# A third probability buffer, a second head-output buffer, raw weights in the keys' tile, and the first keys copied by ScalarE, in a two-layer hybrid attention kernel

## The chip, the cores and the metric

The kernel runs on one core of a Trainium2 chip. Its five engines each work through their own queue in order: TensorE (PE: matrix products, with its weight loads shown as PEld), VectorE (DVE), ScalarE (ACT), GpSimd (POOL) and SyncE (SP), which here only issues DMAs. They wait for one another through semaphores. The metric is the device time of one execution in microseconds (us); lower is better.

## The reference

A backbone of two layers over 512 latent tokens (8 rows of 64) and 256 context tokens, 1024 channels wide. Each layer normalises and modulates its input, projects it once, and runs two attentions side by side: a neighbourhood attention (8 heads of 64, window 8 x 16, relative bias, plus all context keys) and a grouped-query attention (8 query heads, 2 key heads). Each is gated and projected, and both are merged and go through an output projection:

```python
qa = _rmsnorm(hs(a_q, NA_HEADS), q_norm_a)
ka = _rmsnorm(hs(a_k, NA_HEADS), k_norm_a)
a_att = _na_latent(qa, ka, va, cka, cva, rpb, rows)
qb = _rope_2d(_rmsnorm(hs(b_q, GQA_Q_HEADS), q_norm_b), pos_row, pos_col)
b_att = _gqa_latent(qb, k_all, v_all)
# _attend: p = softmax(q k^T / 8); out = p v
# _merge:
o_a = (a_att * silu(a_z)) @ w_o_a
o_b = (b_att * silu(b_z)) @ w_o_b
merged = sigmoid(g_a) * o_a + sigmoid(g_b) * o_b
x_new = x + gate_x * (merged @ w_out)
```

Layer 0 also updates the context tokens (their own attention and projections); layer 1 does not.

## The kernel before

**Products.** Large projections are done to float32 accuracy as three products of rounded parts, high by high, high by low and low by high (L467, L468, L469). A weight tile is loaded raw by SP (256 KB, 128x512), ScalarE casts the high part `whi` (L452, L437), and GpSimd or VectorE subtracts it to get `wlo` (L454, L440). Activations are split in the same way; for the gated attention outputs the parts are `gah`/`gal` and `gbh`/`gbl` (L714 ScalarE, L715 subtraction). Attention products take pairs of float16 tiles.

**Stages of a layer.** Keys, values and queries of the neighbourhood attention; its eight heads; keys, values and queries of the grouped-query attention; its eight heads; then the merge and the output projection. Products of other projections ("fill") are put between the heads' products, so that TensorE has work while the softmax of a head runs elsewhere: gates `zt`/`za`, the first output projection with `w_o_a` (its pieces are emptied from PSUM by VectorE at L750 into `tg`), and, at the end, the second with `w_o_b`.

**The neighbourhood stage.** `na_first(h)` stages head h's keys: `stage_k` copies two halves of 64x1536 float16 values from the large tile `ka` into `kk` (L920, three buffers), and the scores read `kk`. In layer 0 the fill around it is a gate's projection into `za`, whose halves ScalarE (L668) and VectorE (L670) empty.

**The grouped-query stage.** A head has four blocks of 128 queries. For a block TensorE writes scores of 128x768 into PSUM (L928, L929); VectorE finds the maxima and copies the scores into a tile `p` (L1209); ScalarE takes the exponential into `p` (L1210) and casts a float16 part `h` (L898); VectorE (blocks 0 and 2) or GpSimd (blocks 1 and 3) subtracts for the second part (L899); SP transposes both by DMA into `ht` (L903). `p` is free again when L899 is done. In layer 0 a block of context queries follows (L947, `ct`). Then the head's values: twelve products `pst<-ht,vb` (L1226, L1227), a copy and a sum into a tile `ho` (L885, L886), and `zb = zb * ho` (L890). The tile `ho` has one buffer. `divide` (L908, L910, L911) applies the softmax sums. Head h's values come after head h+1's scores, so head 7's come last.

**Buffers.** `NP_GQ = (2, 4)` gives layer 0 two and layer 1 four `p` tiles. Raw weight tiles have three buffers; inside an attention stage every second one comes from an extra set in the stage's pool instead, three buffers in the neighbourhood stages and layer 0's grouped-query stage, two in layer 1's (`raw_tile`, `more_raw`). The grouped-query keys fill only the first half of the large tile `gk`.

**Order.** A scheduler places instructions on every engine from the program text and the buffers, so a change of buffers moves instructions far away from it. No order is written out by hand.

Of the kernel before, what the change touches and what calls it, by code (L numbers as in the profile page):

```python
# [27 lines left out]
STAGE_T = (1, 2)  # L28
NP_GQ = (2, 4)
NH_GQ = (3, 4)  # L30
NT_NA = 2
P_LOG = 9.7
# [42 lines left out]
def hybrid_kernel(es: ExitStack, tc, x, ctx, cvec, w_ada, w_ada0, small, gvec, w_in, w_o_a, w_o_b, w_out,  # L75
# [13 lines left out]
    def nm(s):  # L89
        uid[0] += 1  # L90
        return f"{s}_{uid[0]}"
# [464 lines left out]
    def turn(y, npair, dst, t, perm, g):  # L556
# [10 lines left out]

        todo = []

        def pair(hi, lo, x, g):  # L570
# [67 lines left out]
    def layer(l, hx, nxt, start):  # L638
# [114 lines left out]
        pairs = lambda name: big(name).bitcast(F16).rearrange("p (x j n) -> p x j n", x=2, j=4)  # L753
        kav = pairs("ka")
        k_to = ("k", kav[:, 0], kav[:, 1])
        if first:
# [48 lines left out]
        w = load_w(W, C_AV, 512, KT, mix_lo)  # L805
        za = big("za")
        ti, te = za[:, 0:2048].rearrange("p (h n) -> p h n", h=8), za[:, 2048:3072].rearrange("p (h n) -> p h n", h=8)
        nc.sync.dma_start(ti, bias_int[l].rearrange("h p n -> p h n"))
        nc.sync.dma_start(te, bias_edge[l].rearrange("h p n -> p h n"))

# [6 lines left out]
        for t in range(6):  # L817
            tok_proj(w, 512, a_hx, t, evac_va)
            if t == 3:
# [8 lines left out]
        qav = pairs("qa")  # L828
        w = load_w(W, C_AQ, 512, KT, mix_lo, own=hp["p"])
        fill = fill_chunks(C_AZ, lambda: za, None, True, mix_lo) + fill_chunks(C_BZ, None, zs, True, mix_lo)  # L830
        gates = []
# [4 lines left out]
        for t in range(qt):  # L836
            tok_proj(w, 512, a_hx, t, evac_na(("q", qav[:, 0], qav[:, 1]), True, gq, YB if first else 4))
            if t == 0:
                split_va()
            run(bg, per_bg)  # L840
# [7 lines left out]
        if True:  # L848
# [29 lines left out]
            def head_out(po, e, dst, eng=None, back=None):  # L878

                n = dst.shape[-1]  # L880
                m, o = 64 * e, 64 * (1 - e)
                t1 = att["p"].tile([128, 512], F32, tag="ho", name=nm("ho"), bufs=1)
                a = t1[m:m + 64, :n]
                if back is None:
                    S.copy(a, po[o:o + 64, :n])  # L885
# [4 lines left out]
                (eng or G).tensor_tensor(dst, dst, a, ALU.mult)  # L890
# [25 lines left out]

            def stage_k(src, j, e, to):

                for half in range(2):
                    V.tensor_copy(rows(to, half), rows(src, e)[:, :, j, :])  # L920

            def q_pair(src, e, j):
                return src[:, e, j, :]

            def scores(ps, q, kh, kl, cuts):
# [8 lines left out]
            def ctx_scores(q, kh, kl, ct, late=True):  # L934
# [6 lines left out]
                V.tensor_reduce(mx, pss.rearrange("p (i n) -> p i n", i=2), AX, ALU.max, negate=True)  # L941
                dq = gq_dq if late else na_dq[:, l:l + 1]
                V.tensor_scalar(mx, mx, dq, P_LOG if late else 0.0, ALU.mult, ALU.add)
                p = p_tile()
# [47 lines left out]
            def load_bias(h):  # L992
                nc.sync.dma_start(bint[:, 0:256], b_int[l][h])
                for i in range(2):
                    nc.sync.dma_start(bedg[64 * i:64 * i + 64, 128 * i:128 * i + 128],
                                        b_edge[l][h, 64 * i:64 * i + 64])

            turns = big("ht").bitcast(F16)

            def na_scores(h, q, kh, kl):  # L1000
# [3 lines left out]
                for i in range(4):  # L1004
# [4 lines left out]
                    else:  # L1009
# [11 lines left out]
                    V.tensor_tensor_reduce(p[:, :512], pss, bedg if i == 0 else bint, na_ndq[:, l:l + 1], 3e38,  # L1021
                                           ALU.add, ALU.min, mx[:, 0:1])
# [34 lines left out]
            def pipeline(fill, spread, scores_of, values_of, last=None, bg=[]):  # L1057
# [16 lines left out]
                run(fill, len(fill))  # L1074

            def na_first(h):
                j, e = h // 2, h % 2
                kk = att["p"].tile([128, 2, 768], F16, tag="kk", name=nm("kk"), bufs=3)
                kh, kl = kk[:, 0], kk[:, 1]
# [33 lines left out]
            vbig = big("vb")  # L1113
            g_inv, g_up = vbig[:, 2952:2954], vbig[:, 2954:2956]
            gq_dq, gq_ndq = vbig[:, 2956:2957], vbig[:, 2957:2958]
            g_abs = vbig[:, 1920:2048].rearrange("p (a d) -> p a d", a=2)
            S.copy(g_abs, gbc)
            head_scales(g_abs, g_inv, g_up)
            V.tensor_scalar(gbc[:, 0, :], gbc[:, 0, :], g_up[:, 0:1], None, ALU.mult)
            V.tensor_scalar(gbc[:, 1, :], gbc[:, 1, :], g_up[:, 1:2], 8.0, ALU.mult, ALU.mult)  # L1120
            V.tensor_tensor(gq_dq, g_inv[:, 0:1], g_inv[:, 1:2], ALU.mult)
            V.tensor_scalar(gq_ndq, gq_dq, -1.0, None, ALU.mult)
            V.tensor_scalar(vbig[:, 2950:2951], g_up[:, 0:1], g_up[:, 1:2], -P_LOG, ALU.mult, ALU.mult)

# [7 lines left out]
            vs = vbig[:, 2944:2946]  # L1132
            kbv = hp["p"].tile([128, 2, 1, 768], F16, name=nm("kb"), bufs=1)
            kb_to = ("k", kbv[:, 0], kbv[:, 1])
            gkt = big("gk").bitcast(F16)[:, 0:3072].rearrange("p (e x n) -> p e x n", e=2, x=2)

# [30 lines left out]
            hp["lag"] = 2  # L1167
            qbv = pairs("qb")
            q_to = ("q", qbv[:, 0], qbv[:, 1])
            fill = in_order(gates[n_na:] + o_chunks("a", prepare, evac_a), first)  # L1170
# [8 lines left out]
            for t in range(qt):  # L1179
# [4 lines left out]
                if t in STAGE_T:  # L1184
                    e = STAGE_T.index(t)
                    stage_k(kbv, 0, e, gkt[:, e])

# [7 lines left out]
            if first:  # L1195
                pm["v_for"] = (2,)
            nc.sync.dma_start(zb.rearrange("p (f n) -> p f n", f=4)[:, :, :ntok], zs[:, :, :ntok])
            lift = vbig[:, 2950:2951].to_broadcast([128, 768])

            def gq_scores(q, kh, kl):  # L1200
                ht = att["p"].tile([128, 4, 12, 128], F16, tag="ht", name=nm("ht"), bufs=2)
                r = att["p"].tile([128, 4], F32, tag="r4", name=nm("r4"), bufs=3)
                for i in range(4):
# [4 lines left out]
                    mx = sp.tile([128, 2], F32, tag="mx", name=nm("mx"), bufs=8)  # L1208
                    V.tensor_tensor_reduce(p, pss, lift, gq_ndq, 3e38, ALU.add, ALU.min, mx[:, 0:1])  # L1209
                    S.activation(p, pss, AF.Exp, bias=mx[:, 0:1], scale=gq_dq, accum_out=r[:, i:i + 1])  # L1210
                    turned(p, 768, ht[:, i], G if i in SPLIT_POOL else V)
# [19 lines left out]
            def gq_first(h):  # L1231
                kh, kl = gkt[:, h // 4, 0], gkt[:, h // 4, 1]
                q = q_pair(qbv, h % 2, h // 2)
                ht = gq_scores(q, kh, kl)
# [344 lines left out]
```

## Time and profile before

| | us |
|---|---|
| median of 3 runs | 1122.98 |
| lowest, highest | 1122.5, 1125.72 |
| profiled execution | 1123.93 |
| its span | 1121.6 |
| mean granted TensorE clock | 0.992 |
| DVE, ACT, POOL busy | 784.1, 607.8, 456.8 |

The span is what the trace covers of the profiled execution. In the trace layer 0's neighbourhood heads begin near 153 us, its grouped-query heads end near 538; layer 1's grouped-query heads lie between 930 and 1052. A row of the timeline gives the start, the duration, the engine, the line in the program, the operation, what is written and read, and in brackets how long the engine stood idle before it and what released it. A row of the waits view gives, for one engine and line and one releaser, the idle time in total, the number of waits and the longest.

### The profile page before, as it was taken

Reading aid. Unit: us, or ns where it says so; the run is one execution under the profiler, and the core shown is the slowest. Engines: PE = TensorE matmul, PEld = TensorE weight load, DVE = VectorE, ACT = ScalarE, POOL = GpSimd, SP = SyncE. Lnnn points to the kernel's source line nnn. Section 1 sums busy time; section 2 is a strip of 40 time slices with the busy share of each in tenths; the row PEclk is TensorE's granted clock in tenths of the full one; section 3 lists DMA queues with packets and bytes.
Section 4 is the critical chain, followed back from the end, with each engine's and each line's share of the span. In section 5 each row is a group of like instructions: output and inputs, shape, how many; then the busy total and the mean of one; then the engine's idle time right before and its main releaser. Section 6 shows DMA issues by size and latency. Waiting matters only on the chain. (4 is left out here: it accounts for less than half of the span.)

```text
span 1121.6 us, 16972 instructions
## 1 busy us (share of the span) xinstructions
PE 1073.7 (96%) x5672; PEld 842.3 (75%) x5672; DVE 784.1 (70%) x1667; ACT 607.8 (54%) x1219; POOL 456.8 (41%) x393
## 2 busy tenths in 40 slices
PE   8999989999999999889999999999999998999898
PEld 5688877777888867666888778887666886756687
DVE  4667998976379488656577866477886776677473
ACT  5465448776433566766230274544797436688231
POOL 1054314654245155465322535332554453575421
PEclk8999999999999999989999999999999999999999
DMA  9665334754544499789533533753564437789643
GB/s 358 205 177 170 103 100 102 149 132 100 169 131 131 118 223 204 160 215 245 169 116 102 195 122 95 231 155 109 138 144 115 139 107 189 177 234 233 156 144 93
DMA packets 244464, 178.20 MB, mean 159 GB/s; under 512 B 160285, under 2 KB 210329, under 8 KB 242713
## 3 DMA queue, kind: packets, MB, share of 16 engines
q1 hardware_dynamic: 236896, 162.61, 53.5%
q0 software_dynamic: 2368, 7.87, 2.1%
q10 hardware_dynamic: 5112, 6.66, 1.9%
q8 instruction: 44, 0.72, 0.3%
q14 instruction: 44, 0.35, 0.1%
HBM read 118.86 MB, written 20.47 MB: 124 GB/s over the span
## 5 line engine op out<-in xcount | busy, mean ns | idle before, releaser
L899 POOL TENSOR_TENSOR h<-p,h 128x256 f16<-128x256 f32 (+2 forms) x104 | 109.8, 1062 | 175.0 <-ACT h L898 140.1
L467 PE MATMUL psf<-hx,whi 128*128 128x512 f32 (+1 forms) x360 | 138.9, 386 | 2.6 <-DVE za L670 1.5
L454 POOL TENSOR_TENSOR wlo<-raw,whi 128x512 fp32r<-128x512 f32 x70 | 97.9, 1407 | 97.6 <-ACT whi L452 67.6
L469 PE MATMUL psf<-hx,wlo 128*128 128x512 f32 (+1 forms) x360 | 137.3, 382 | 0.0
L468 PE MATMUL psf<-hx,whi 128*128 128x512 f32 (+1 forms) x360 | 136.7, 380 | 0.0
L468 PE MATMUL psx<-wlo,hx 128*128 128x512 f32 (+1 forms) x328 | 120.8, 369 | 1.3 <-DVE wlo L440 1.3
L467 PE MATMUL psx<-whi,hx 128*128 128x512 f32 (+1 forms) x328 | 120.9, 370 | 0.0
L469 PE MATMUL psx<-whi,hx 128*128 128x512 f32 (+1 forms) x328 | 120.3, 367 | 0.0
L452 ACT CAST whi<-raw 128x512 fp32r<-128x512 f32 x136 | 80.7, 618 | 57.8 <-DMA raw<-in_w_in_dram 33.5
L440 POOL TENSOR_TENSOR wlo<-raw,whi 128x512 fp32r<-128x512 f32 x40 | 54.6, 1367 | 137.5 <-ACT whi L437 99.0
L437 ACT CAST whi<-raw 128x512 fp32r<-128x512 f32 x88 | 54.0, 624 | 91.9 <-PE psx L469 30.4
L540 POOL TENSOR_TENSOR ss<-ss,ehalf 128x8 f32<-128x8 f32 (+2 forms) x40 | 65.8, 1648 | 87.6 <-DVE ss L537 86.2
L898 ACT CAST h<-p 128x256 f16<-128x256 f32 (+2 forms) x136 | 81.7, 616 | 10.5 <-DVE p L857 4.3
L1210 ACT ACTIVATE p<-pss,mx,vb 128x768 f32<-128x768 f32 x64 | 63.4, 993 | 43.7 <-DVE mx L1209 42.4
L1209 DVE CUSTOM_DVE_ANT_0 p<-pss,vb 128x768 f32<-128x768 f32 x64 | 64.2, 1013 | 31.6 <-PE pss L929 26.7
L454 DVE TENSOR_TENSOR wlo<-raw,whi 128x512 fp32r<-128x512 f32 x66 | 69.5, 1061 | 18.9 <-ACT whi L452 18.7
L467 PEld LDWEIGHTS psf<-hx,whi 128*128 128x128 f32 x360 | 67.9, 189 | 16.0 <-ACT zt L668 1.9
L469 PEld LDWEIGHTS psf<-hx,wlo 128*128 128x128 f32 x360 | 67.8, 188 | 12.2
L468 PEld LDWEIGHTS psf<-hx,whi 128*128 128x128 f32 x360 | 68.0, 189 | 11.1
L468 PEld LDWEIGHTS psx<-wlo,hx 128*128 128x128 f32 x328 | 62.0, 189 | 11.8 <-DVE wlo L440 2.2
L467 PE MATMUL psx<-hx,whi 128*128 128x256 f32 (+1 forms) x208 | 69.3, 333 | 0.4 <-DVE za L670 0.4
L469 PEld LDWEIGHTS psx<-whi,hx 128*128 128x128 f32 x328 | 61.9, 189 | 10.1 <-DVE hx L383 0.4
(350 smaller groups left out, 2904.2 us busy)
## 6 DMA issues: line engine op xcount, KB each, us to landing
raw<-in_w_in_dram SPq DMA_DIRECT2D x168, 256.0 KB, 3.1
rawb<-in_w_ada_dram SPq DMA_DIRECT2D x48, 256.0 KB, 3.1
raw<-in_w_out_dram SPq DMA_DIRECT2D x32, 256.0 KB, 2.9
tg<-gs SPq DMA_DIRECT2D x4, 1536.0 KB, 7.3
rawx<-in_w_ada_dram SPq DMA_DIRECT2D x4, 1024.0 KB, 11.4
rawy<-in_w_ada_dram SPq DMA_DIRECT2D x4, 1024.0 KB, 10.7
gs<-zt ACTq DMA_DIRECT2D x16, 256.0 KB, 2.5
raw<-in_w_o_a_dram SPq DMA_DIRECT2D x16, 256.0 KB, 3.2
```

The lines of the kernel that those rows point to most:

```text
L437: S.copy(hi[:, :n], raw[:, :n])
L440: e.tensor_tensor(lo[:, :n], raw[:, :n], F(hi[:, :n]), ALU.subtract)
L452: S.copy(hi, raw)
L454: lo_eng(i).tensor_tensor(lo, raw, F(hi), ALU.subtract)
L467: T.matmul(ps, lhs[0], rhs[0], start=first, stop=False)
L468: T.matmul(ps, lhs[0], rhs[1], start=False, stop=False)
L469: T.matmul(ps, lhs[1], rhs[0], start=False, stop=last)
L540: G.tensor_tensor(ss, ss, ehalf[:, :n], ALU.pow)
L898: S.copy(h[:, 0], p[:, :n])
L899: eng.tensor_tensor(h[:, 1], p[:, :n], h[:, 0], ALU.subtract)
L1209: V.tensor_tensor_reduce(p, pss, lift, gq_ndq, 3e38, ALU.add, ALU.min, mx[:, 0:1])
L1210: S.activation(p, pss, AF.Exp, bias=mx[:, 0:1], scale=gq_dq, accum_out=r[:, i:i + 1])
```

## The change

Five things take effect. Layer 0's grouped-query stage gets three `p` tiles instead of two. In both layers the extra raw weight tiles of that stage are three slices of the unused half of the tile `gk`, no longer tiles of the stage's pool; in layer 1 that is one more than before, and the slices exist before the stage opens. `ho` has two buffers in both attentions. Head 0's two key copies in layer 0 are done by ScalarE (`S.copy`). One small product on `gcol` is split into two. The diff adds another path for `NA_PAIRS` or `GQ_PAIRS` being false; both are true for both layers, so none of it is built. Lines of the changed kernel have other numbers: L946 is the old L920, L980 and L981 the old L928 and L929, L1301 and L1302 the old L1209 and L1210, L771 the old L750.

```diff
-NP_GQ = (2, 4)
+NP_GQ = (3, 4)
+NA_PAIRS = (True, True)
+GQ_PAIRS = (True, True)
...
-                return more_raw["p"].tile([128, 512], F32, tag="rawp", name=nm("raw"), bufs=more_raw["bufs"])
+                return more_raw["p"]()
...
-        V.tensor_tensor(gcol[:, 48:52], gcol[:, 48:52], flat(up), ALU.mult)
+        for l in range(2):
+            if NA_PAIRS[l]:
+                c = 48 + 2 * l
+                V.tensor_tensor(gcol[:, c:c + 2], gcol[:, c:c + 2], up[:, l], ALU.mult)
...
-                t1 = att["p"].tile([128, 512], F32, tag="ho", name=nm("ho"), bufs=1)
+                t1 = att["p"].tile([128, 512], F32, tag="ho", name=nm("ho"), bufs=2 if (na_pairs if att["w"] == 512 else gq_pairs) else 1)
...
-            def stage_k(src, j, e, to):
+            def stage_k(src, j, e, to, eng):
 
                 for half in range(2):
-                    V.tensor_copy(rows(to, half), rows(src, e)[:, :, j, :])
+                    eng(rows(to, half), rows(src, e)[:, :, j, :])
...
-                more_raw["p"], more_raw["bufs"] = att["p"], 3 if width == 512 or first else 2
+                pool, turn = att["p"], [0]
+
+                def own_tile():
+                    return pool.tile([128, 512], F32, tag="rawp", name=nm("raw"), bufs=3)
+
+                def part_of_gk():
+                    turn[0] += 1
+                    o = 1536 + 512 * (turn[0] % 3)
+                    return gkb[:, o:o + 512]
+                if width == 512 and na_pairs:
+                    more_raw["p"] = own_tile
+                elif width == 768 and gq_pairs:
+                    more_raw["p"] = part_of_gk
...
-                stage_k(kav, j, e, kk)
-                q = q_pair(qav, e, j)
+                if na_pairs:
...
+                    stage_k(kav, j, e, kk, S.copy if first and h < 1 else V.tensor_copy)
+                    q = q_pair(qav, e, j)
...
-            gkt = big("gk").bitcast(F16)[:, 0:3072].rearrange("p (e x n) -> p e x n", e=2, x=2)
+            gkb = big("gk")
+            if gq_pairs:
...
+                gkt = gkb.bitcast(F16)[:, 0:3072].rearrange("p (e x n) -> p e x n", e=2, x=2)
```

How the instructions move, at three places.

**The start of layer 0's neighbourhood heads, VectorE.** `kk_1530` before and `kk_1531` after are head 0's keys, the next two tiles those of heads 1 and 2. Before:

```order
L990 MEMSET bedg_1524 64x128
L920 COPY kk_1530<-ka_161 64x1536 x2
L920 COPY kk_1697<-ka_161 64x1536 x2
L920 COPY kk_1909<-ka_161 64x1536 x2
L670 SCALAR_TENSOR_TENSOR za_778<-za_778,psf_1619 128x512
```

After, on VectorE:

```order
L1059 MEMSET bedg_1525 64x128
L946 COPY kk_1698<-ka_161 64x1536 x2
L946 COPY kk_1910<-ka_161 64x1536 x2
L691 SCALAR_TENSOR_TENSOR za_779<-za_779,psf_1620 128x512
L459 TENSOR_TENSOR wlo_1684<-raw_1680,whi_1682 128x512
```

and on ScalarE, where L597 is the last scaling of queries and L689 the gate's part:

```order
L689 ACTIVATE za_779<-psx_1474 128x256
L597 ACTIVATE qa_1032<-pst_1501,gcol 64x4x128 x2
L946 COPY kk_1531<-ka_161 64x1536 x2
L689 ACTIVATE za_779<-psf_1620 128x512
L457 CAST whi_1676<-raw_1674 128x512
```

Head 0's two copies stand on ScalarE ahead of the gate's part; VectorE keeps four in a row.

**Layer 0's grouped-query stage where the fill turns to `w_o_a`, VectorE.** The rows with `p` and `mx` are the maxima of head 6's score blocks, `tg` and `psf` the first pieces of the fill. Before:

```order
L899 TENSOR_TENSOR h_5596<-p_5592,h_5596 128x768
L1209 ISA p_5605,mx_5606<-pss_5600,vb_3447 128x768
L1209 ISA mx_5606 128x1
L750 SCALAR_TENSOR_TENSOR tg_5363<-tg_5363,psf_5367 128x512
L1209 ISA p_5618,mx_5619<-pss_5613,vb_3447 128x768
L1209 ISA mx_5619 128x1
L750 SCALAR_TENSOR_TENSOR tg_5363<-tg_5363,psf_5381 128x256
```

After:

```order
L925 TENSOR_TENSOR h_5588<-p_5584,h_5588 128x768
L937 SCALAR_TENSOR_TENSOR zb_4123<-psv_5671,vb_3448,zb_4123 64x256
L1301 ISA p_5597,mx_5598<-pss_5592,vb_3448 128x768
L1301 ISA mx_5598 128x1
L1301 ISA p_5610,mx_5611<-pss_5605,vb_3448 128x768
L1301 ISA mx_5611 128x1
L771 SCALAR_TENSOR_TENSOR tg_5356<-tg_5356,psf_5360 128x512
L1301 ISA p_5623,mx_5624<-pss_5618,vb_3448 128x768
```

Two maxima now stand between the subtraction and the first emptying; on TensorE the twelve value products that stood ahead of the fill's first piece come four pieces later, and the block `pss_5618` stands between the first piece and the second. At the stage's end TensorE's last score block of head 7 moves from before head 6's values to after them.

**The end of layer 1's grouped-query stage, TensorE.** `pst_10997` before and `pst_10978` after are head 7's values; `psx` and `psf` with `gbh` or `gbl` are products with `w_o_b`. Before:

```order
L468 MATMUL psf_10964<-gal_10595,whi_10840 128x512
L469 MATMUL psf_10964<-gah_10594,wlo_10842 128x512
L1226 LDWEIGHTS vb_9273
L1226 MATMUL pst_10997<-ht_10858,vb_9273 128x512
L1227 LDWEIGHTS vb_9273
```

After:

```order
L474 MATMUL psx_11145<-gbh_10963,wlo_11072 128x512
L472 MATMUL psx_11145<-gbh_10963,whi_11076 128x512
L473 MATMUL psx_11145<-gbl_10964,whi_11076 128x512
L1319 LDWEIGHTS vb_9264
L1319 MATMUL pst_10978<-ht_10839,vb_9264 128x512
L1320 LDWEIGHTS vb_9264
```

Fifty-three products with `w_o_b`, heads 0 to 5's share, now stand ahead of head 7's values; before, five did, and after the values one such product is left ahead of those that read head 7's own share. SP issues the loads of `w_o_b` ahead of head 7's first transposition, where two of them stood directly ahead of its last; GpSimd's three subtractions for `gbl` now precede head 7's last subtraction.

More of the change, by code (lines that the diff above doesn't have):

```diff
@@ L568, in turn @@
         todo = []
+        if not isinstance(dst, tuple):
+            if perm and t in (0, 3):
+                x = pt.rearrange("p (j s n) -> p j s n", j=npair, s=2)
+                d = dst[:, :, 0:512].rearrange("p j (s n) -> p j s n", n=64)
+                if t == 0:
+                    d = d[:, :, 0:3:2, :]
+                else:
+                    x, d = x[:, :, ::-1, :], d[:, :, 1:8:6, :]
+            else:
+                x = pt.rearrange("p (j n) -> p j n", j=npair)
+                d = dst[:, :, cuts[0][2]:cuts[0][2] + 128]
+            if g is None:
+                S.copy(d, x)
+            else:
+                S.activation(d, x, AF.Copy, scale=g)
+            return
         def pair(hi, lo, x, g):
@@ L753, in layer @@
         pairs = lambda name: big(name).bitcast(F16).rearrange("p (x j n) -> p x j n", x=2, j=4)
-        kav = pairs("ka")
-        k_to = ("k", kav[:, 0], kav[:, 1])
+        whole = lambda name: big(name).rearrange("p (j n) -> p j n", j=4)
+        na_pairs, gq_pairs = NA_PAIRS[l], GQ_PAIRS[l]
+        kav = (pairs if na_pairs else whole)("ka")
+        k_to = ("k", kav[:, 0], kav[:, 1]) if na_pairs else kav
         if first:
@@ L818, in layer @@
             tok_proj(w, 512, a_hx, t, evac_va)
-            if t == 3:
+            if t == 3 and na_pairs:
                 behind(ON_ACT, scale_bias)
@@ L915, in rows, with k_tile, split_k, split_q @@
                 return a[64 * half:64 * half + 64]
-            def stage_k(src, j, e, to):
+            def stage_k(src, j, e, to, eng):
                 for half in range(2):
-                    V.tensor_copy(rows(to, half), rows(src, e)[:, :, j, :])
+                    eng(rows(to, half), rows(src, e)[:, :, j, :])
             def q_pair(src, e, j):
                 return src[:, e, j, :]
+            def k_tile(e):
+                kh = att["p"].tile([128, 768], F32R, tag=f"kh{e}", name=nm("kh"), bufs=1)
+                kl = att["p"].tile([128, 768], F32R, tag=f"kl{e}", name=nm("kl"), bufs=1)
+                V.tensor_scalar(rows(kl, 1 - e).rearrange("p (a b) -> p a b", b=128),
+                                rows(ident, 1 - e).unsqueeze(1).to_broadcast([64, 6, 128]),
+                                0.0, None, ALU.mult)
+                return kh, kl
+            def split_k(src, e, kh, kl, dup):
+                k = rows(src, e)
+                V.tensor_copy(rows(kh, e), k)
+                S.copy(rows(kh, 1 - e), k)
+                (G if dup else V).tensor_tensor(rows(kl, e), k, F(rows(kh, e)), ALU.subtract)
+                if dup:
+                    S.copy(rows(kl, 1 - e), F(rows(kl, e)))
+            def split_q(src, e):
+                n = 768 if first else 512
+                qs = att["p"].tile([128, n], F32R, tag=f"qs{e}", name=nm("qs"), bufs=1)
+                q = rows(src, e)[:, :n]
+                S.copy(rows(qs, e), q)
+                V.tensor_tensor(rows(qs, 1 - e), q, F(rows(qs, e)), ALU.subtract)
+                return qs
             def scores(ps, q, kh, kl, cuts):
@@ L1132, in layer @@
             vs = vbig[:, 2944:2946]
-            kbv = hp["p"].tile([128, 2, 1, 768], F16, name=nm("kb"), bufs=1)
-            kb_to = ("k", kbv[:, 0], kbv[:, 1])
-            gkt = big("gk").bitcast(F16)[:, 0:3072].rearrange("p (e x n) -> p e x n", e=2, x=2)
+            gkb = big("gk")
+            if gq_pairs:
+                kbv = hp["p"].tile([128, 2, 1, 768], F16, name=nm("kb"), bufs=1)
+                kb_to = ("k", kbv[:, 0], kbv[:, 1])
+                gkt = gkb.bitcast(F16)[:, 0:3072].rearrange("p (e x n) -> p e x n", e=2, x=2)
+                gkt = [(gkt[:, e, 0], gkt[:, e, 1], gkt[:, e]) for e in range(2)]
+            else:
+                kb_to = kbv = hp["p"].tile([128, 1, 768], F32, name=nm("kb"), bufs=1)
+                gkt = R(gkb).rearrange("p (a n) -> p a n", a=4)
+                gkt = [(gkt[:, 2 * e], gkt[:, 2 * e + 1]) for e in range(2)]
             def evac_bkv(t, ps):
@@ L1197, in layer @@
             nc.sync.dma_start(zb.rearrange("p (f n) -> p f n", f=4)[:, :, :ntok], zs[:, :, :ntok])
+            if not gq_pairs:
+                V.memset(vbig[:, 2950:2951], -P_LOG)
             lift = vbig[:, 2950:2951].to_broadcast([128, 768])
```

80 lines of the change are left out of this document (50 added, 30 removed).

## The prediction

> **What bounds the kernel now.** I read the page's busy times first, then what TensorE waits for, then its timeline at each long wait.
>
> ```profile
> PE 1073.7 (96%) x5672; PEld 842.3 (75%) x5672; DVE 784.1 (70%) x1667; ACT 607.8 (54%) x1219; POOL 456.8 (41%) x393
> ```
>
> TensorE (PE) is busy for 1073.7 of 1121.6 us, so only its 48 us of idle time, and any time in which it runs slowly, can be won. The change takes no matmul away. The waits view of PE says what ended the idle time (us in total, times, longest):
>
> ```profile
> PE pst L1226 <- DMA ht<-h: 7.6, 6, 2.7
> PE psf L467 <- DVE tg L750: 5.8, 5, 2.9
> PE pss L928 <- DVE kk L920: 2.4, 1, 2.4
> ```
>
> The first two belong to the grouped-query stage: values waiting for transposed probabilities, and fill products waiting until VectorE has emptied their PSUM bank. The third is the start of layer 0's neighbourhood stage. The timeline of PE has the single waits (start, duration, instruction, idle before and its releaser):
>
> ```profile
> 155.79 0.22 PE L928 MATMUL pss<-kk,qa 128*128 128x128 f16 x1 [2.39 <-DVE kk L920]
> 157.32 0.28 PE L467 MATMUL psx<-hx,whi 128*128 128x256 f32 x1
> 157.44 0.28 PE L468 MATMUL psx<-hx,whi 128*128 128x256 f32 x1
> 158.80 0.49 PE L467 MATMUL psf<-hx,whi 128*128 128x512 f32 x1 [0.97 <-DVE za L670]
> 457.18 0.61 PE L963 MATMUL psv<-ct,vb 128*128 128x256 f16 x4 [2.75 <-DMA ct<-h]
> 497.69 0.58 PE L467 MATMUL psf<-gah,whi 128*128 128x256 f32 x1 [2.87 <-DVE tg L750]
> 498.07 0.41 PE L468 MATMUL psf<-gal,whi 128*128 128x256 f32 x1
> 498.29 0.41 PE L469 MATMUL psf<-gah,wlo 128*128 128x256 f32 x1
> 531.15 0.39 PE L1226 MATMUL pst<-ht,vb 128*128 128x512 f16 x1 [0.92 <-DMA ht<-h]
> 531.38 0.38 PE L1227 MATMUL pst<-ht,vb 128*128 128x512 f16 x1
> 951.29 0.38 PE L1226 MATMUL pst<-ht,vb 128*128 128x512 f16 x1 [2.71 <-DMA ht<-h]
> 1042.51 0.50 PE L467 MATMUL psf<-gah,whi 128*128 128x512 f32 x1 [1.52 <-DVE tg L750]
> 1048.12 0.39 PE L1226 MATMUL pst<-ht,vb 128*128 128x512 f16 x1 [2.55 <-DMA ht<-h]
> ```
>
> Two of these cost more than the wait. Equal 128x256 products start 0.12 us apart at 157.32 and 0.22 us apart at 498.07. The table of windows (length, busy time of PE, PEld, DVE, ACT, POOL, then the granted clock) shows why:
>
> ```profile
> 496.00:500.00 4.00, 2.31 (x11) 2.31 (x12) 2.56 (x5) 2.76 (x5) 1.32 (x2) 0.55 0.93 225
> 500.00:504.00 4.00, 4.00 (x14) 2.87 (x14) 3.04 (x5) 2.51 (x4) 2.16 (x2) 0.60 0.72 83
> 1048.00:1052.00 4.00, 3.88 (x13) 1.70 (x13) 0.00 (x0) 0.00 (x0) 2.84 (x3) 0.67 0.77 258
> ```
>
> The clock falls to 0.55 and 0.60 after the wait at 497.69. From there to 500, 2.3 us run at 0.12/0.22 of the pace and lose 1.0; the next 4 us at 0.60 lose 1.6; together 2.6 us. After 1048.12, 4 us at 0.67 lose 1.3. So the stall at 497.69 costs 2.87 + 2.6 = 5.5, and layer 1's tail 1.52 + 2.55 + 1.3 = 5.4. The waits of 2.75 and 2.71 are followed by no such pace.
>
> By the Trainium skill ("TensorE: Matmul & The Clock Gate", Part 1) the clock halves after an idle window of about 3.4 us that runs freely. By that rule taken as a threshold no single wait here would lower it, and the two stalls would be worth 3.9 us less; the rows differ, since 2.87 was enough, so the measurement decides.
>
> **The first keys (−1.25 us).** Two of the six copies L920 leave VectorE (DVE) for ScalarE (ACT).
>
> ```profile
> L920 DVE COPY kk<-ka x6: 552/556/1609, 152.6 to 157.5; 64x1536 f16<-64x1536 f16 x6
> 152.50 1.29 POOL L454 TENSOR_TENSOR wlo<-raw,whi 128x512 fp32r<-128x512 f32 x1 [12.20 <-PE psx L468]
> 144.95 1.39 ACT L576 ACTIVATE qa<-pst,gcol 64x512 f16<-64x512 f32 x2
> 151.17 0.60 ACT L668 ACTIVATE za<-psf 128x512 f32<-128x512 f32 x1 [4.83 <-PE psf L469]
> ```
>
> No ACT copy of this shape is in the trace. Its nearest row is 64x512 in 0.70 us, so three times the columns cost at most 2.1 us, and two cost 4.2; if a part of the 0.70 is fixed, less. ACT is free from 146.34 to 151.17, so 4.2 us is hidden there, even at the upper bound. If that cover were gone, the za read at 151.17 would be late, but PE waits for its VectorE half only at 158.80. PE's 2.39 goes. It does not come off whole: PE then reaches the product at 158.80 early, and that needs za (L670), which stands behind the copies. The six end at 157.5 + 0.55, 5.45 us after 152.6, where six undisturbed ones take 6 x 0.556 = 3.3; the extra 2.1 falls on the first, 1.61 us long, and its successor, while GpSimd (POOL) subtracts (L454). If the four left pay that extra, za ends at 152.6 + 4 x 0.556 + 2.1 + 0.7 = 157.6 rather than just before 158.80, and the end moves by some 1.2. If not, by up to 3.1. I take −1.25, with 0 and −3.1 as ends, because POOL's subtraction stays where it is.
>
> By the Trainium skill ("SBUF — State Buffer", Who interferes with whom) VectorE and GpSimd share one port pair as an exclusive lock, which ScalarE does not use. That speaks against the −3.1: the lock would now hit the next copies. By it the term is −1.25, without it −3.1.
>
> **Third probability buffer in layer 0 (−2.3, then +2.2).** VectorE's waits in 375 to 545 us bound what a buffer can do:
>
> ```profile
> DVE p L1209 <- PE pss L929: 17.5, 9, 8.9
> DVE p L1209 <- POOL h L899: 4.4, 6, 1.1
> ```
>
> The maxima (L1209) wait 17.5 us for scores, and only 4.4 us for a free buffer. So the buffer itself is worth little; what matters is where it lets work move. At the stall:
>
> ```profile
> 486.87 7.17 POOL L715 TENSOR_TENSOR gal<-za,gah 128x768 fp32r<-128x768 f32 x4
> 493.04 2.94 DVE L899 TENSOR_TENSOR h<-p,h 128x768 f16<-128x768 f32 x1
> 496.01 1.02 DVE L1209 CUSTOM_DVE_ANT_0 p<-pss,vb 128x768 f32<-128x768 f32 x1
> 496.95 0.68 DVE L750 SCALAR_TENSOR_TENSOR tg<-tg,psf 128x512 f32<-128x512 f32 x1
> ```
>
> The fill's first piece was finished at 497.69 - 2.87 = 494.8, but its emptying (L750) stood behind a subtraction of 2.94 and a maximum of 1.02. In the new order the subtraction comes earlier, and PE has two products and one score block more (0.5 + 0.9 us) between the last maximum's scores and the second piece; the maximum (1.0) and the emptying (0.7) then leave a wait of about 0.5. Against that, twelve value products (12 x 0.22 = 2.6, by the spacing at 531.15) no longer stand ahead of the first piece, and its later parts wait for gal, which POOL delivers at 1.8 us a quarter. The old order met gal's last quarter with 0.26 us of waiting:
>
> ```profile
> 494.09 0.50 PE L468 MATMUL psf<-gal,whi 128*128 128x512 f32 x1 [0.26 <-POOL gal L715]
> ```
>
> so the new one waits 0.26 + 2.6 = 2.9 there, in parts. The stall thus goes from 0.26 + 5.5 to 2.9 + 0.5 = 3.4, split into waits too short for a slow clock: −2.3. Ends: −5.2 if only the 0.5 is left, +0.3 if the clock falls all the same.
>
> Then the tail of the stage. The last score block ended at 514.5 and its transposed copy was there at 531.15, 16.6 us later:
>
> ```profile
> 514.22 0.27 PE L929 MATMUL pss<-gk,qb 128*128 128x256 f16 x1
> 517.46 1.02 DVE L1209 CUSTOM_DVE_ANT_0 p<-pss,vb 128x768 f32<-128x768 f32 x1 [1.08 <-POOL h L899]
> 522.76 1.90 SPq L903 DMA_TRANSPOSE ht<-h  x1
> ```
>
> In the new order head 6's values come before this block, so that only 10.0 us of PE work lie between it and head 7's values (24 products of 512 columns at 0.23, 24 of 256 at 0.12, 1.6 for the context and the divisors), where 14.1 did. The chain without queues is 1.0 (maximum) + 1.2 (exponential) + 0.8 (cast) + 1.7 (POOL's subtraction) + 8.4 (522.76 to 531.15) = 13.1, and the 1.5 MB load of a gate stands ahead of the transposition in both orders. A wait of 3.1 replaces 0.92: +2.2. Ends: if the landing took only the 4.8 us from 1043.28 to 1048.12, −0.9; if the chain stayed at 16.6 us, a wait of 6.6 and 2.6 of slow clock, +8.3.
>
> **Raw weights in the keys' tile (−2.4 and −1 in layer 1).** In layer 1 this gives a third extra buffer, and loads of w_o_b move ahead of the transpositions that they delayed. SyncE's queue and what follows at the tail:
>
> ```profile
> 1041.43 1.02 SPq L449 DMA_DIRECT2D raw<-in_w_o_b_dram  x2
> 1043.28 2.18 SPq L903 DMA_TRANSPOSE ht<-h  x1
> 1046.68 4.15 POOL L715 TENSOR_TENSOR gbl<-zb,gbh 128x512 fp32r<-128x512 f32 x3
> 1052.36 0.58 ACT L885 COPY ho<-pst 64x512 f32<-64x512 f32 x1 [6.26 <-PE pst L1227]
> 1054.42 0.62 ACT L714 CAST gbh<-zb 128x512 fp32r<-128x512 f32 x1 [1.49 <-DVE zb L890]
> ```
>
> With the weights there early, PE does 53 products of o_b (0.23 us each, 12.2) ahead of head 7's values. The chain from the last score (1031.75, by the row below) to 1048.12 was 16.4 us; less the waits of 1.52 and 2.55 it was covered by 12.3 us of work. Now the cover is 14 fill products, the divisors and the 53: 3.2 + 0.5 + 12.2 = 15.9. The wait shrinks to about 0.5.
>
> ```profile
> 1031.48 0.27 PE L929 MATMUL pss<-gk,qb 128*128 128x256 f16 x1
> ```
>
>  What is late next: o_b's last quarter needs head 7 itself, through the rows 1052.36 to 1054.42 + 0.62, 2.7 us after the values; those 53 products hid it, and only one is left (0.2). New wait 2.5. So 5.4 becomes 3.0 with no slow clock: −2.4. Ends: −2.9 without the 0.5, and +3.0 if POOL's gbl (4.15), now ahead of the last subtraction, delays the transposition by its length and the clock falls again. At the stage's start, the 2.71 at 951.29 stood behind three loads issued since 944.32; they leave, −1, ends −2.7 and 0.
>
> At nothing: in layer 0 the keys' tile replaces three buffers by three, and loads go out earlier into time in which PE has no wait; the second output buffer removes ACT waits that PE doesn't see; the split gcol product is one more tiny instruction. Their cover is PE's queue of products.
>
> **Sum.** −1.25 − 2.3 + 2.2 − 2.4 − 1 = −4.8. The profiled execution took 1123.93 (span 1121.6), so it would take 1119.2; it lay 0.95 above the median of 1122.98, from which the same sum gives 1118.2 us, the prediction.
>
> **Rivals.** (1) The waits only move: the third buffer does nothing, since 17.5 of the maxima's waits are for scores, and o_b's products hide either one wait or the other. Only the keys count: 1122.98 - 1.25 = 1121.7. For it: the 2.5 that reappears. Against it: two stretches of slow clock that a divided wait avoids. (2) Slower: head 7's last transposition is late in both layers. Price +8.3 and +3.0, less 1.25 + 2.3 + 1: +6.8, 1129.7 us. It decides once the two tails lose 8 us more than now. For it: the cover cut to 10.0, a chain that measured 16.6. Against it: 1.08 of that chain was the wait for the buffer. (3) All stalls go: −1.25 − 5.2 + 0 − 2.9 − 2.7 = −12.1, 1110.9. For it: each has its named cause in the old order. Against it: gal and head 7 still come late.
>
> **How the numbers follow.** Forecast 0.42 (its own range 1115 to 1121.5), waits only move 0.22, slower 0.21, all stalls go 0.13, other 0.02. A change within 0.3% (3.4 us) can't be told from none. Of the forecast 0.31 lies below 1119.6; with 0.13 and a little of the rest, faster 0.46. The same takes 0.11 of it and most of the first rival, 0.30; slower 0.24. The range reaches to the third rival and takes in most of the slower one: 1111 to 1128.
>
> **What would show it.** Head 0's scores without a wait on kk and za near 157.6; at the fill's first emptying short waits for gal and no granted clock under 0.9; before head 7's values of layer 0 a wait of 2 to 4; in layer 1 under 1 there and 2 to 3 at the first product of o_b's last quarter. A clock that falls at a tail, or new waits elsewhere of 3 us together, would make the prediction wrong.

## The result, and the profile after

The change made the kernel slower: 1131.9 us median (1131.5 to 1135.12) against 1123.68 beside it, a ratio of 1.0077 (95% interval 1.0053 to 1.0102). The prediction was 1118.2, with a range of 1111 to 1128. The profiled execution took 1131.5, its span is 1129.6. The page's busy times after:

```profile
PE 1077.3 (95%) x5672; PEld 844.1 (75%) x5672; DVE 793.4 (70%) x1666; ACT 608.7 (54%) x1221; POOL 454.5 (40%) x393
```

TensorE has the same 5672 products and is busy 3.6 us longer, most of it slow clock (mean granted clock 0.989 for 0.992); the other 4.4 us of the span are idle time. To see where, I take instructions that both traces have, in TensorE's timeline. Before, the first softmax divisor of layer 0's grouped-query heads, the transposition of `y` after the stage, and the first scores of layer 1:

```profile
397.76 0.43 PE L910 MATMUL psv<-ident,r 128*128 128x128 f32 x2 [1.24 <-DVE r L908]
639.62 1.09 PE L375 MATMUL pst<-ident,y 128*128 128x128 f32 x8 [1.28 <-DVE y L366]
777.16 0.23 PE L928 MATMUL pss<-kk,qa 128*128 128x128 f16 x1 [1.69 <-DVE qa L577]
```

After, the same three, the waits over 2.3 us, and one of 1.91 that follows two of them:

```profile
158.35 0.50 PE L472 MATMUL psf<-hx,whi 128*128 128x512 f32 x1 [2.37 <-DVE za L691]
397.50 0.43 PE L936 MATMUL psv<-ident,r 128*128 128x128 f32 x2 [1.19 <-DVE r L934]
441.29 0.39 PE L1319 MATMUL pst<-ht,vb 128*128 128x512 f16 x1 [2.54 <-DMA ht<-h]
491.13 0.79 PE L472 MATMUL psf<-gah,whi 128*128 128x512 f32 x1 [3.28 <-ACT zt L689]
497.64 0.58 PE L980 MATMUL pss<-gk,qb 128*128 128x512 f16 x1 [3.21 <-ACT p L1004]
504.02 0.38 PE L980 MATMUL pss<-gk,qb 128*128 128x512 f16 x1 [1.91 <-ACT p L1302]
537.49 0.39 PE L472 MATMUL psf<-gah,whi 128*128 128x256 f32 x1 [3.07 <-DVE tg L771]
648.78 1.09 PE L380 MATMUL pst<-ident,y 128*128 128x128 f32 x8 [1.05 <-DVE y L371]
786.35 0.23 PE L980 MATMUL pss<-kk,qa 128*128 128x128 f16 x1 [1.68 <-DVE qa L598]
1069.73 0.50 PE L472 MATMUL psf<-gbh,whi 128*128 128x512 f32 x1 [2.66 <-ACT gbh L735]
```

| place | before | after | difference |
|---|---|---|---|
| first divisor, layer 0's grouped-query heads | 397.76 | 397.50 | −0.26 |
| transposition of `y` after the stage | 639.62 | 648.78 | +9.16 |
| first scores of layer 1 | 777.16 | 786.35 | +9.19 |
| end of the span | 1121.6 | 1129.6 | +8.0 |

So all of the loss, 9.4 us, lies behind 397 and ahead of the transposition of `y`, in layer 0, and layer 1 gives 1.2 back. Three of the new waits stand together between 487 and 504. The windows there (length, PE, PEld, DVE, ACT, POOL busy, granted clock) show TensorE idle for much of it and slow in the rest:

```profile
488.00:492.00 4.00, 0.87 (x2) 0.78 (x3) 4.00 (x1) 3.44 (x7) 4.00 (x3) 0.85 0.95 371
492.00:496.00 4.00, 2.43 (x6) 1.46 (x6) 4.00 (x1) 0.00 (x0) 4.00 (x3) 0.72 1.01 420
496.00:500.00 4.00, 2.36 (x8) 1.64 (x8) 2.63 (x7) 3.42 (x8) 1.73 (x3) 0.71 1.02 380
500.00:504.00 4.00, 2.12 (x8) 0.85 (x8) 3.94 (x7) 1.11 (x3) 0.37 (x1) 0.87 0.65 146
```

In the first two windows VectorE's column reads 4.00 with one instruction. The timeline names it, with what GpSimd and ScalarE did beside it:

```profile
487.09 9.20 DVE L996 TENSOR_SCALAR mx<-mx,vb 128x2 f32<-128x2 f32 x1
528.32 0.23 DVE L996 TENSOR_SCALAR mx<-mx,vb 128x2 f32<-128x2 f32 x1
486.30 1.28 POOL L459 TENSOR_TENSOR wlo<-raw,whi 128x512 fp32r<-128x512 f32 x1
487.53 7.13 POOL L736 TENSOR_TENSOR gal<-za,gah 128x768 fp32r<-128x768 f32 x4
494.61 1.65 POOL L925 TENSOR_TENSOR h<-p,h 128x768 f16<-128x768 f32 x1
485.47 3.03 ACT L735 CAST gah<-za 128x768 fp32r<-128x768 f32 x4
490.70 0.38 ACT L689 ACTIVATE zt<-psf 128x256 f32<-128x256 f32 x1
```

The scaling of a context block's maxima, two columns, takes 9.20 us where it takes 0.23 at 528. It starts while GpSimd subtracts, and ends at 496.29, when GpSimd's unbroken run ends at 494.61 + 1.65 = 496.26. The exponential of that block (ACT L1004) waits for it, and TensorE for that. The wait of 3.28 has another cause: the gate's last emptying (zt) stands behind four gah casts on ScalarE, and the twelve value products that TensorE had at this point before now come later. The wait of 1.91 follows a subtraction and two maxima that start late after the hold. The wait of 3.07 is of the first kind again; here VectorE's subtraction of a weight's low part, 0.68 us at 512.69, is held:

```profile
531.26 4.93 DVE L459 TENSOR_TENSOR wlo<-gk,whi 128x512 fp32r<-128x512 f32 x1
529.16 2.77 POOL L925 TENSOR_TENSOR h<-p,h 128x768 f16<-128x768 f32 x2
531.89 3.75 POOL L459 TENSOR_TENSOR wlo<-raw,whi 128x512 fp32r<-128x512 f32 x3
```

### The profile page after: what moved, and what is told of

The parts are those of the page before. It is cut to its first block, busy times and chain, and to the rows that moved or that the text cites. A ratio compares the mean times of both kernels' runs of the same rounds, so it can differ in the third digit from the quotient of the medians.

```text
span 1129.6 us, 16970 instructions
## 1 busy us (share of the span) xinstructions
PE 1077.3 (95%) x5672; PEld 844.1 (75%) x5672; DVE 793.4 (70%) x1666; ACT 608.7 (54%) x1221; POOL 454.5 (40%) x393
## 5 line engine op out<-in xcount | busy, mean ns | idle before, releaser
L925 POOL TENSOR_TENSOR h<-p,h 128x256 f16<-128x256 f32 (+2 forms) x104 | 109.7, 1062 | 172.4 <-ACT h L924 141.6
L442 ACT CAST whi<-raw 128x512 fp32r<-128x512 f32 x88 | 53.9, 624 | 94.3 <-PE psx L474 30.8
L457 ACT CAST whi<-raw 128x512 fp32r<-128x512 f32 x116 | 69.6, 619 | 49.8 <-DMA raw<-in_w_in_dram 28.8
L1301 DVE CUSTOM_DVE_ANT_0 p<-pss,vb 128x768 f32<-128x768 f32 x64 | 63.9, 1013 | 32.6 <-PE pss L981 32.2
L1302 ACT ACTIVATE p<-pss,mx,vb 128x768 f32<-128x768 f32 x64 | 63.3, 992 | 43.3 <-DVE mx L1301 43.0
L474 PEld LDWEIGHTS psx<-whi,hx 128*128 128x128 f32 x328 | 61.9, 189 | 10.0 <-DVE hx L388 0.4
L472 PEld LDWEIGHTS psx<-whi,hx 128*128 128x128 f32 x328 | 61.9, 189 | 9.6 <-issue 0.2
```

Of the source, the lines that this page charges most:

```text
L442: S.copy(hi[:, :n], raw[:, :n])
L457: S.copy(hi, raw)
L472: T.matmul(ps, lhs[0], rhs[0], start=first, stop=False)
L474: T.matmul(ps, lhs[1], rhs[0], start=False, stop=last)
L925: eng.tensor_tensor(h[:, 1], p[:, :n], h[:, 0], ALU.subtract)
L1301: V.tensor_tensor_reduce(p, pss, lift, gq_ndq if gq_pairs else -1.0, 3e38, ALU.add, ALU.min, mx[:, 0:1])
```

## The experiments

Each is compared with the kernel before on the same chip. Theory A: GpSimd's run holds VectorE up. Theory B: the new order starves TensorE in any case. Theory C: the earlier weight loads crowd the transpositions.

| run | what it is | ratio to before | 95% interval |
|---|---|---|---|
| full change | | 1.0077 | 1.0053 to 1.0102 |
| e8 | full change again | 1.0067 | 1.0043 to 1.0092 |
| e7 | keys on ScalarE only | 1.0001 | 0.9986 to 1.0015 |
| e2 | keys, raw weights in gk | 0.9989 | 0.9964 to 1.0015 |
| e3 | the same and three p buffers | 1.0051 | 1.0030 to 1.0072 |
| e4 | e2 and two ho buffers | 1.0031 | 1.0008 to 1.0055 |
| e1 | full change, maxima in PSUM | 1.0039 | 1.0020 to 1.0057 |
| e5 | e1, gal on VectorE | 1.0025 | 1.0007 to 1.0042 |
| e9 | e5, one more subtraction off VectorE | 1.0019 | 1.0000 to 1.0037 |
| e11 | e5, two gah casts on GpSimd | 0.9965 | 0.9942 to 0.9988 |
| e6 | before, gal on VectorE | 0.9944 | 0.9924 to 0.9963 |
| e10 | e6, maxima in PSUM | 0.9939 | 0.9913 to 0.9966 |

**e1: one operand moved.** The maxima go through two spare PSUM columns; the order of every engine stays, up to layer 1's last projection.

```diff
-                pss = ps_score()
+                both = ps_score(1024 if late else 512)
+                pss = both[:, :512]
...
-                V.tensor_reduce(mx, pss.rearrange("p (i n) -> p i n", i=2), AX, ALU.max, negate=True)
+                raw_mx = both[:, 512:514] if late else mx
+                V.tensor_reduce(raw_mx, pss.rearrange("p (i n) -> p i n", i=2), AX, ALU.max, negate=True)
...
-                V.tensor_scalar(mx, mx, dq, P_LOG if late else 0.0, ALU.mult, ALU.add)
+                V.tensor_scalar(mx, raw_mx, dq, P_LOG if late else 0.0, ALU.mult, ALU.add)
```

> The full change, with one operand moved: the maxima of a context block are reduced into two unused PSUM columns of the same score tile, so that the scaling behind them (128x2) reads PSUM and no longer SBUF. Nothing is left out; the order of all engines stays that of the full change up to layer 1's last projection. Theory A (GpSimd's unbroken run of gal holds up a VectorE instruction that works from SBUF to SBUF, 9.20 us for one of 0.23, and TensorE starves behind it): that instruction takes under 0.5 us, the waits of 3.28, 3.21 and 1.91 us shrink to under 2 together, and the time falls by 6 to 9 us to 1123 to 1126. Theory B (the order itself: the third probability buffer delays what TensorE needs, with or without the long instruction): within 2 us of 1131.9. Theory C (earlier weight loads crowd the transpositions): within 2 us of 1131.9.

The ratio fell to 1.0039, so about half of the loss went by the middle values; the intervals of e1 and of the full change still overlap. The timeline of that run, VectorE, GpSimd and TensorE:

```profile
485.33 0.22 DVE L998 TENSOR_SCALAR mx<-pss,vb 128x2 f32<-128x2 f32 x1
493.17 2.84 DVE L925 TENSOR_TENSOR h<-p,h 128x768 f16<-128x768 f32 x1 [2.04 <-ACT h L924]
485.76 7.14 POOL L736 TENSOR_TENSOR gal<-za,gah 128x768 fp32r<-128x768 f32 x4
492.87 1.65 POOL L925 TENSOR_TENSOR h<-p,h 128x768 f16<-128x768 f32 x1
489.36 0.50 PE L472 MATMUL psf<-gah,whi 128*128 128x512 f32 x1 [3.28 <-ACT zt L689]
498.84 0.38 PE L980 MATMUL pss<-gk,qb 128*128 128x512 f16 x1 [3.29 <-ACT p L1304]
533.48 0.38 PE L472 MATMUL psf<-gah,whi 128*128 128x256 f32 x1 [3.04 <-DVE tg L771]
```

The scaling takes 0.22 us and is done before the run; but it ran just ahead of gal here, so this row alone doesn't say that a PSUM source is never held. A later instruction from SBUF to SBUF, the subtraction L925, is held instead (2.84 for 0.94) while GpSimd works on without a break behind gal, and TensorE waits 3.29 behind it. Since the order is the same, the two traces can be laid side by side: from the product behind zt to the one behind tg, TensorE needs 46.36 us in the full change (491.13 to 537.49) and 44.12 here. So the held scaling cost 2.2 us there. The 6 to 9 us expected were too many; another instruction is held instead, and the waits of 3.28 and 3.04 stay. B stays possible for the rest.

**e2, e3, e4: parts of the change.** All three have the keys on ScalarE, the split gcol product and the raw weights in gk. e2 has `NP_GQ = (2, 4)` and one `ho` buffer, e3 `(3, 4)` and one, e4 `(2, 4)` and two. No run has a p or ho buffer without the raw weights in gk.

> Before, with the first keys on ScalarE and the raw weights in the keys' tile; layer 0 keeps two probability buffers and all attentions one head-output buffer. VectorE's order around the fill's turn to w_o_a is that of before. Theory A: no long instruction in the gal run, so 1121 to 1123.5. Theory B (third probability buffer): the same, 1121 to 1123.5. Theory C (loads): most of the loss is already here, 1128 or more.

> The full change with one head-output buffer, so with the third probability buffer. Theory B: the loss is here, 1130 to 1133. Theory A: the time goes by whether a VectorE instruction from SBUF to SBUF falls into the gal run. In the order the context scaling of head 5 stands further ahead of the fill's first emptying, so it should escape: 1121 to 1126. Theory C: 1128 or more.

> The full change with two probability buffers in layer 0, so with the second head-output buffer. Theory B: no loss, 1121 to 1124. Theory A: the context scaling stands right ahead of the last instructions before the fill's first emptying; if it is late enough to miss gal, 1121 to 1125, if not, it is long again and the time is 1128 or more; the duration of that instruction and the time must go together. Theory C: 1128 or more.

e2 is no slower, so C falls. e3 and e4 are, each with one buffer more (the intervals of e2 and e4 just overlap): each buffer alone reorders the stage. Rows of VectorE and GpSimd, of e3:

```profile
491.99 1.02 DVE L1302 CUSTOM_DVE_ANT_0 p<-pss,vb 128x768 f32<-128x768 f32 x1 [0.27 <-PE pss L982]
492.94 4.00 DVE L926 TENSOR_TENSOR h<-p,h 128x768 f16<-128x768 f32 x1
488.95 7.16 POOL L737 TENSOR_TENSOR gal<-za,gah 128x768 fp32r<-128x768 f32 x4
```

and of e4:

```profile
489.45 7.04 DVE L997 TENSOR_SCALAR mx<-mx,vb 128x2 f32<-128x2 f32 x1
489.33 7.12 POOL L737 TENSOR_TENSOR gal<-za,gah 128x768 fp32r<-128x768 f32 x4
```

In e3 the scaling escaped, as expected, but the subtraction fell into gal instead (4.00 for 0.95), and its 1129.47 us is nearer to B's 1130 to 1133 than to A's 1121 to 1126. In e4 the scaling is held for the length of gal, and 1127.83 us is what A had for that case, not B's 1121 to 1124. B in its form "the third probability buffer" falls with e4, which lacks it; in a wider form it doesn't, since TensorE's wait for zt is there with 2.98 us in e4 and 1.31 in e3. The maximum at 491.99, which reads PSUM, runs in its usual 1.02 us in the middle of gal.

**e5 and e6: the run taken away.** In layer 0 the gal subtractions go to VectorE, in e1's kernel (e5) and in the kernel before (e6):

```diff
-            hilo(za, gated["a"], range(4))
+            hilo(za, gated["a"], range(4), V if first else G)
```

> The first experiment's kernel (context maxima in PSUM), and in layer 0 the four gal subtractions on VectorE instead of GpSimd; nothing is left out, and the order of the other instructions changes in few places. Theory A (GpSimd's gal run holds VectorE up): with the run gone no VectorE instruction there takes over 1.5 us, the wait of 3.29 us near 499 and the slow clock behind it go, 1123 to 1126 against the first experiment's ratio of 1.0039. Theory B (the order itself): the fill still meets the gate's last copy (ACT zt) 3.3 us early and the head's maxima late, so within 1.5 us of the first experiment.

> Before, with the four gal subtractions of layer 0 on VectorE. Theory A: the subtraction of 2.94 us at 493 falls to about 1 us and the wait of 2.87 us at 497.69, with the slow clock behind it (2.6 us), shrinks: 3 to 5.5 us faster than before, ratio 0.995 to 0.997. Rival: VectorE's additional 4 x 0.95 us delay the maxima as much as GpSimd's run did: no difference, or slower by up to 3 us.

e6 has a clear gain: 1117.97 us, ratio 0.9944, a little more than expected, though VectorE has more to do. Behind 487 us the order differs from the kernel before in places on VectorE, ScalarE and GpSimd, so the gain need not be the hold's alone. Its rows at the old stall:

```profile
492.99 0.95 DVE L899 TENSOR_TENSOR h<-p,h 128x768 f16<-128x768 f32 x1
494.71 0.38 PE L928 MATMUL pss<-gk,qb 128*128 128x512 f16 x1 [1.25 <-ACT p L1210]
496.00:500.00 4.00, 3.49 (x20) 2.87 (x19) 2.41 (x5) 2.17 (x5) 1.67 (x2) 1.00 1.20 355
```

The subtraction is back to 0.95, the wait of 2.87 is gone, and the clock stays at 1.00. e5 fell only to 1.0025, which can't be told from e1: 1127.77 us lies outside A's 1123 to 1126 and within 1.5 us of e1, as B had it. The wait near 499 shrank to 1.25, but its rows show the 3.28 as it was, and a second hold at the tail:

```profile
491.12 0.50 PE L472 MATMUL psf<-gah,whi 128*128 128x512 f32 x1 [3.28 <-ACT zt L689]
532.07 0.66 PE L936 MATMUL psv<-ident,r 128*128 128x128 f32 x2 [3.89 <-DVE r L934]
524.99 5.95 DVE L459 TENSOR_TENSOR wlo<-gk,whi 128x512 fp32r<-128x512 f32 x1
```

**e7: the keys alone.** `NP_GQ`, `ho` and the raw weights as before.

> Before, with head 0's two key copies on ScalarE (and the gcol product in two), nothing else. The prediction's term says 1.25 us faster (ratio 0.9989). The rival from the trace of the full change says 0 to 0.5 us: the wait of 2.39 us on kk is replaced by one of 2.4 us on za, and this one is followed by 4 us at a granted clock near 0.6. Both lie close to what can be measured; the profile decides by the wait at za and the clock in 156 to 164 us.

```profile
157.76 0.50 PE L473 MATMUL psf<-hx,whi 128*128 128x512 f32 x1 [2.37 <-DVE za L692]
160.00:164.00 4.00, 4.00 (x14) 2.59 (x14) 3.89 (x16) 3.79 (x10) 0.96 (x2) 0.68 0.66 197
```

The rows are the rival's: the wait moved from kk to za, in one piece, and the clock fell to 0.68 behind it. There is no gain that can be measured; the interval alone would still hold the 1.25 us.

**e8, e9, e10.** e8 is the full change again. e9 is e5 with the last quarter of w_o_a split on GpSimd alone, e10 is e6 with e1's PSUM columns.

```diff
-st["w"] = load_w2(src, 256 * i, 4, pool_lo if br == "b" and i == 0 else mix_lo)
+st["w"] = load_w2(src, 256 * i, 4, pool_lo if (br == "b" and i == 0) or (first and br == "a" and i == 3) else mix_lo)
```

> The full change once more, beside the kernels below on one chip. All theories: slower than before, ratio 1.005 to 1.010. Theory A: a VectorE instruction of about 9 us again beside GpSimd's gal run, near 487 us, since the order on both engines is fixed.

> The kernel with the maxima in PSUM and gal on VectorE, and in layer 0 all low parts of the last quarter of w_o_a on GpSimd, so that VectorE has no subtraction of that kind (5.95 us beside GpSimd's run near 525) ahead of the stage's tail. The order changes in more places than before. Theory A: no VectorE instruction over 3 us in 480 to 545 us and the wait of 3.89 us before head 7's values goes with the slow clock behind it: ratio 0.997 to 1.000. Theory B: the tail waits for something else instead and the ratio stays within 0.0015 of 1.0025.

> Before, with gal of layer 0 on VectorE and the context maxima in PSUM; the order is that of the kernel with gal on VectorE alone. Theory A: the context scalings fall from up to 1.29 us to 0.2 us, but TensorE did not wait on them there, so ratio 0.993 to 0.996, within 0.002 of that kernel's 0.9944.

In e8 the scaling is held for 9.20 us again, to the hundredth:

```profile
486.69 9.20 DVE L996 TENSOR_SCALAR mx<-mx,vb 128x2 f32<-128x2 f32 x1
```

e9 missed A's 0.997 to 1.000 and stayed by 1.0025, as B had it. Its order changed in many more places than e1's. The hold and the wait of 3.89 went, but others came, one in the stage and one at layer 1's start:

```profile
518.80 0.38 PE L980 MATMUL pss<-gk,qb 128*128 128x512 f16 x1 [2.59 <-ACT p L1304]
655.12 0.50 PE L473 MATMUL psx<-wlo,hx 128*128 128x512 f32 x1 [1.31 <-POOL wlo L445]
```

e10, at 1116.88 us, has the lowest median of all runs and beats both kernels; it lies within its expectation, and its interval overlaps e6's.

e10 also gives the comparison that decides how far theory A goes. e5 and e10 have the same two edits, gal on VectorE and the maxima in PSUM, one on the changed kernel and one on the kernel before. So between them stands the change alone, without gal on GpSimd on either side: 1.0025 against 0.9939, 0.9% apart, no less than the full change's 0.7 to 0.8%. GpSimd's gal run costs the kernel before as well, and taking it away on both sides doesn't make the change harmless.

**e11: the other half.** e5 with two of the four gah casts on GpSimd.

```diff
-                    S.copy(R(dst[0][:, f, n0:n1]), sv[:, f, n0:n1])
+                    (G.tensor_copy if f in hi_g else S.copy)(R(dst[0][:, f, n0:n1]), sv[:, f, n0:n1])
...
+            hilo(za, gated["a"], range(4), V if first else G, hi_g=(2, 3) if first else ())
```

> The kernel with the maxima in PSUM and gal on VectorE, and in layer 0 two of the four gah casts on GpSimd, so that two fewer ScalarE casts (0.76 us each) stand ahead of the gate's last emptying (zt), for which the fill's first product waits 3.28 us. Order theory: that wait falls by the two casts, to 1.6 to 1.9 us, and the granted clock behind it stays above 0.9; the ratio falls from 1.0025 by 0.001 to 0.003. If the wait stays near 3.3 us, the casts were not what held zt up, and the ratio stays within 0.001 of 1.0025.

```profile
489.24 0.50 PE L472 MATMUL psf<-gah,whi 128*128 128x512 f32 x1 [1.81 <-ACT zt L689]
492.00:496.00 4.00, 3.89 (x13) 2.04 (x12) 3.57 (x9) 2.47 (x6) 2.46 (x3) 0.63 1.01 392
```

The wait fell from 3.28 to 1.81, the two casts' length, so the casts held zt up. The ratio fell to 0.9965, by 0.006 where 0.001 to 0.003 were expected and more than two casts are worth; the order moved too, and the tail's wait of 3.89 is gone in this run. The clock dropped all the same, against the expectation. With gal, the maxima and two casts moved, the change's buffers stand in a kernel that is faster than before; but e10, without them, has the lower median.

## Why the prediction was wrong

**The first keys.** The mechanism was right: two ScalarE copies hidden ahead of za, no wait of the scores, and four copies left that pay GpSimd's price:

```profile
147.00 2.96 ACT L946 COPY kk<-ka 64x1536 f16<-64x1536 f16 x2
153.30 4.27 DVE L946 COPY kk<-ka 64x1536 f16<-64x1536 f16 x4
160.00:164.00 4.00, 4.00 (x13) 2.82 (x12) 3.86 (x17) 3.84 (x11) 0.68 (x1) 0.61 0.71 207
```

4.27 is 4 x 0.556 + 2.05, as the step had it. What failed is the size: the two waits of 2.39 and 0.97 became one of 2.37, and 4 us at 0.61 lose 1.6 us, more than the 1.25. I had said of the other stalls that a divided wait keeps the clock, and didn't turn it round here.

**The fill's first emptying, the step that failed.** The prediction had the stall go "from 0.26 + 5.5 to 2.9 + 0.5 = 3.4, split into waits too short for a slow clock". It went to 3.28 + 3.21 + 1.91 = 8.4 with a slow clock, 0.71 to 0.87 over four windows, which loses about 1.8 us more (an estimate from TensorE's busy time in them). That is some 4.4 us more than the old stall where 2.3 less were forecast, about half of the 13 us by which the sum missed. The 2.9 was nearly right in size, by a wrong releaser: TensorE met ScalarE's queue, not gal; e11 shows that. The 0.5 was wrong. I quoted the subtraction of 2.94 us with gal's 7.17 us above it, and took it for a delay that goes when the subtraction moves. It is a hold that strikes other VectorE instructions too: copies, scalings and subtractions from SBUF to SBUF, though not all of that kind (e1's reciprocal of 128x2 at 490.96 takes 0.17 us in the middle of gal). In the new order that was a two-column scaling, for 9.20 us. For the keys I had charged exactly this price, and not here.

What is shown of the loss is a part: e1, with the order kept, makes the held scaling one cause of the loss, worth 2.2 us in the trace and some 0.3% of the ratio. The rest of the loss is not explained by gal on GpSimd, since e5 stays 0.9% behind e10. What its trace shows in that place is the wait of 3.28, which comes of the order and which e11 shortens, and the tail's wait of 3.89 behind the other held subtraction; how much each is worth stays open.

**The stage's tail.** The +2.2 was to be a late transposition. No wait over 0.4 us stands ahead of head 7's values after; the wait of 3.07 there is a held VectorE subtraction once more. By the Trainium skill ("SBUF — State Buffer", Who interferes with whom) the loser of the port pair that VectorE and GpSimd share blocks for the whole instruction of the winner. The rows of the scaling go further: 9.20 us, through the end of one GpSimd instruction, four more and a sixth.

**The third buffer.** It did what it says: VectorE's waits for a free p (4.4 us before) are not in the view after. No run has it alone; e3, which adds it to e2, is the slower of the two. The waits for scores, 17.5 us, which had suggested that it is worth little, are 18.6 after.

**Layer 1.** The step said −3.4, and 1.2 came. Head 7's values don't wait longer than 0.4 us, the stall of 2.71 at the start is gone, and the new wait of 2.5 for gbh is there with 2.66. What was left out: that wait is followed by 4 us at 0.69, 1.2 us, and short waits for zt (0.73 and 0.97) came at the stage's start.

**The rivals.** Faster had 0.46. The slower rival had the sign, but its mechanism, late transpositions in both tails, did not happen. The slower outcome came in part by a mechanism that was on the page and not among the rivals. What stays open is how much of the loss is the order rather than the hold, in e3, e4 and the full change; each has both.

## What to carry to other kernels

Ahead of a change of buffers or order, list GpSimd's long unbroken runs, and look in the new order at which VectorE copies, scalings and subtractions from SBUF to SBUF fall beside them: each can cost up to what is left of the run, however small it is. Taking the run away was worth more than any buffer here (e6). To learn whether such a run is why a change loses, take it away on both sides, as e5 and e10 do; a cure that helps the old kernel as much explains nothing of the difference. And count a slow clock behind a wait near 2.4 us as possible: the 2.37 behind the first keys cost 1.6 us more in the full change and nothing more in e3.

## What the runs showed of the hardware

The hold goes on over the borders of GpSimd's instructions in the full change (through six of them, 9.20 us), but in e1 the subtraction held at 493.17 ended at 496.0, while GpSimd was still at work, so VectorE sometimes gets in between.

The clock after like waits is not the same. The wait for ct at 457 left it alone before (2.75 us), and not in e7, where it was shorter. The wait in e7, the window behind it, then the window of the kernel before:

```profile
456.06 0.99 PE L1021 MATMUL psv<-ct,vb 128*128 128x256 f16 x4 [2.60 <-DMA ct<-h]
456.00:460.00 4.00, 3.94 (x14) 2.74 (x15) 3.74 (x10) 2.24 (x5) 2.34 (x2) 0.57 1.19 227
```

```profile
456.00:460.00 4.00, 2.82 (x16) 2.23 (x17) 3.90 (x9) 2.27 (x5) 3.35 (x2) 1.00 1.03 255
```

In a set of 27 runs the kernel before spread from 1117.8 to 1129.9 us. Slow stretches that come or not, at 1 to 2 us each, would give such a spread; that they do was not tried.
